# Newton iterations for reciprocal square roots: the iterate in columns of the PSUM tile just summed

## The chip, the cores and the metric

The kernel runs on one core of a Trainium2 chip. Its engines are TensorE (PE; its weight loads are shown apart as PEld), VectorE (DVE), ScalarE (ACT) and GpSimd (POOL); SyncE (SP) issues most DMAs. The metric is the device time of one execution in microseconds (us), the median of several runs. A profile is one more execution, taken by the hardware profiler.

## What is computed

Two transformer blocks of two layers each, on 512 tokens of 1024 features, in float32. Reciprocal square roots stand in every normalisation: of the residual stream, of the heads' queries and keys, and of the mixers' outputs. Cut to these:

```
def rmsnorm(x, g):
    xf = x.astype(jnp.float32)
    y = xf * lax.rsqrt(jnp.mean(xf * xf, axis=-1, keepdims=True) + EPS)
    return (y * g.astype(jnp.float32)).astype(x.dtype)

def l2norm(x):
    return x * lax.rsqrt(jnp.sum(x * x, axis=-1, keepdims=True) + EPS)
...
        qa = apply_grid_rope(rmsnorm(qa.reshape(b, s, A_HEADS, A_HEAD_DIM), q_norm_g[l]), cos, sin)
...
        qd = l2norm(qd.reshape(b, s, DN_HEADS, DN_DK)) * (DN_DK ** -0.5)
...
def _memory_cross_attention(h, mem_h, w_q, w_kv, q_norm_g, k_norm_g, w_o):
    q = _rms(_split_heads(h @ w_q, XA_HEADS), q_norm_g)
    mk, mv = _split_cols(mem_h @ w_kv, (XA_HEADS * XA_HD, XA_HEADS * XA_HD))
    mk = _rms(_split_heads(mk, XA_HEADS), k_norm_g)
```

The ten phases follow one another: mix and feed-forward twice (first block), then an even mixer, cross-attention, feed-forward, an odd mixer, cross-attention, feed-forward (second block).

## The kernel before

Activations lie with features on the 128 partitions and the 512 tokens along the free dimension. Each weight piece is split into a high and a low part: ScalarE casts it to whi (L474), GpSimd subtracts to get wlo (`tt` with engine gpsimd, L383), and three matmuls make one product (L487, L490, L491, in `proj`) into the PSUM tiles psb, or ps. Four pieces of each part are in flight (pool `whl`).

A reciprocal root takes this path. Squares are made by ScalarE. `tok_sums` transposes four (or two) 128-token pieces of them on TensorE into a PSUM tile ps (L412), and VectorE adds up each row (L416), so that a token stands on a partition and a root is one column: 4 columns for a norm, up to 32 where several heads and tiles share a chain. `rsqrt` then forms 1/sqrt(scale*x + eps) on VectorE, with a shift and a subtraction on the bits as the first guess and three Newton steps: 12 instructions on 2 to 32 columns, each waiting for the one before. Its working tile is called rsq, its result rc, or nrc for a norm of the residual stream, or rso for the delta rule's output. `spread` (L455) transposes the columns back over all partitions on TensorE. `rs_cols` does sums and root for a head's vectors; where these are of a still unnormalised projection, `r` is the norm, and the sums are first multiplied by its squared root (rc2) and the result by its root (rc).

`Norm.chunk` runs once for each of eight feature tiles of the residual stream; the last call forms the sums, nrc, its square and the spread copy rB (L303), which scales the projections as they leave PSUM (`pad<-psb,rB`, `x<-psb,rB`). There are ten norms, and 64 chains in all: ten of norms, two of rso, 52 of `rs_cols`.

In cross-attention (`_cross`) the root of the queries, rq, scales the row maximum and the exponentials (L1721, ScalarE), which VectorE then divides by their sum (L1726) before TensorE transposes them (L1728); the root of the memory, mrc, scales the values as ScalarE copies them from PSUM (L1699). In mix, two chains of 16 columns (`queries`, first and second group) run beside `solve`, the triangular inverse whose products ntmp and sums N are VectorE's, and beside the attention core, whose exponentials (L956) need the roots. `l2` makes two chains of 32 columns beside the convolution (kq, L697). PSUM tiles come from rings: `pss`, `psf` and `psg` with one to four buffers a phase, psb with two. A scheduler that knows a cost for each instruction orders each engine's instructions ahead of time; the engines then run them in that order.

Of the kernel before, what the change touches and what calls it, by code (L numbers as in the profile page):

```python
# [11 lines left out]
F32 = mybir.dt.float32  # L12
F32R = mybir.dt.float32r
I32 = mybir.dt.int32
AF = mybir.ActivationFunctionType
ALU = mybir.AluOpType
# [4 lines left out]
P = 128  # L21
S = 512
D = 1024
DEPTH = 2
EPS = 1e-6
# [79 lines left out]
NVEC, _ = _vec_layout()  # L105
# [155 lines left out]
class Norm:  # L261
# [10 lines left out]
    def chunk(self, m):  # L272
        k, nc = self.k, self.k.nc
        a = k.actp.tile([P, 2, S], F32R, name="act", tag="act")
        gcol = k.vec(self.g, m)
        nc.scalar.activation(a[:, 0], k.x[m], AF.Copy, scale=gcol)
        lo = nc.vector.scalar_tensor_tensor(a[:, 1], k.x[m], gcol, a[:, 0].bitcast(F32), ALU.mult, ALU.subtract)  # L277
        self.acts[m] = a
        sq = k.nrm.tile([P, S], F32, name="nsq", tag="nsq", bufs=2) if self.n else k.nrm.tile([P, S], F32, name="ssq", tag="ssq")
        if self.first and m in (1, 3, 5):  # L280
            k.tt(sq, k.x[m], k.x[m], ALU.mult, "gpsimd")
        else:
            self.last = lo, nc.scalar.activation(sq, k.x[m], AF.Square)
        self.n += 1

        if self.n == 1:
            self.acc = sq
        elif self.n < 8:
            k.tt(self.acc, self.acc, sq, ALU.add, "vector" if self.first else "gpsimd")
        if self.n == 7:  # L290
            self.sums = k.nrm.tile([P, 2, 4], F32, name="nsum", tag="nsum", bufs=2)
            k.tok_sums(self.sums[:, 0], self.acc)
        if self.n == 8:
            k.tok_sums(self.sums[:, 1], sq)
            k.tt(self.sums[:, 0], self.sums[:, 0], self.sums[:, 1], ALU.add)

            self.rc = k.nrm.tile([P, 4, 1], F32, name="nrc", tag="nrc", bufs=2)
            self.rc2 = k.nrm.tile([P, 4, 1], F32, name="nrc2", tag="nrc2", bufs=2)
            k.rsqrt(self.rc.rearrange("p t c -> p (t c)"), self.sums[:, 0], 1.0 / D, EPS)
            k.tt(self.rc2, self.rc, self.rc, ALU.mult)  # L300
            ps = k.spread(self.rc)
            self.r = k.nrm.tile([P, S], F32, name="rB", tag="rB")
            nc.scalar.copy(self.r, ps)  # L303


class Prog:
# [75 lines left out]
    def tt(self, out, a, b, op, eng="vector"):  # L382
        getattr(self.nc, eng).tensor_tensor(out, a, b, op)  # L383

    def rsqrt(self, out, in_, scale, eps):


        nc = self.nc
        n = out.shape[-1]
        y = self.nrm.tile([P, 2, 32], F32, name="rsq", tag="rsq", bufs=4)  # L390
        v, u = y[:, 0, :n], y[:, 1, :n]
        nc.vector.tensor_scalar(v, in_, scale, eps, ALU.mult, ALU.add)
        nc.vector.tensor_scalar(u.bitcast(I32), v.bitcast(I32), 1, None, ALU.logical_shift_right)
        nc.vector.tensor_scalar(out.bitcast(I32), u.bitcast(I32), -1.0, float(0x5F3759DF), ALU.mult, ALU.add)
        for _ in range(3):
            self.tt(u, out, out, ALU.mult)
            nc.vector.scalar_tensor_tensor(u, u, -0.5, v, ALU.mult, ALU.mult)  # L397
            nc.vector.scalar_tensor_tensor(out, u, 1.5, out, ALU.add, ALU.mult)

    def issue_behind(self, ins, before):  # L400

# [4 lines left out]
    def tok_sums(self, out, sq, view=None, nt=4, psum=None):  # L406


        nc = self.nc
        ps = (psum or self.pss)()  # L410
        for t in range(nt):
            nc.tensor.transpose(ps[:, t * P:(t + 1) * P], sq[:, t * P:(t + 1) * P], self.ident)  # L412
        v = ps[:, :nt * P].rearrange("p (t d) -> p t d", t=nt)
        if view is not None:
            v = view(v)
        nc.vector.tensor_reduce(out, v, AX.X if len(v.shape) == len(out.shape) + 1 else AX.XY, ALU.add)  # L416

    def rs_cols(self, groups, view, ncol, scale, eps, nt=4, psum=None, r=None):

        nc = self.nc
        n = nt * ncol
        rc = self.nrm.tile([P, 32], F32, name="rc", tag="rc", bufs=4)
        sums = self.nrm.tile([P, 32], F32, name="sums", tag="sums", bufs=4)
        ng = 0
        for sq in groups:
            self.tok_sums(sums[:, ng * n:(ng + 1) * n].rearrange("p (t c) -> p t c", t=nt), sq, view, nt, psum)
            ng += 1
        by_tok = lambda t: t[:, :n * ng].rearrange("p (g t c) -> p g t c", g=ng, t=nt)  # L430
        of = lambda t: t.unsqueeze(1).broadcast_to((P, ng, nt, ncol))
        if r is not None:
            self.tt(by_tok(sums), by_tok(sums), of(r.rc2), ALU.mult)
        self.rsqrt(rc[:, :n * ng], sums[:, :n * ng], scale, eps)
        if r is not None:
            self.tt(by_tok(rc), by_tok(rc), of(r.rc), ALU.mult)
        return [rc[:, g * n:(g + 1) * n].rearrange("p (t c) -> p t c", t=nt) for g in range(ng)]

    def all_features(self, v):
# [202 lines left out]
    def _mix(self, l, nm, nxt, mp):  # L642
        nc, tc = self.nc, self.tc
# [87 lines left out]
        ps = self.pss()  # L731
# [5 lines left out]
        ps = self.pss()  # L737
# [26 lines left out]
        ps = self.pss()  # L764
# [10 lines left out]
        ps = self.pss()  # L775
# [490 lines left out]
        rso = mp.tile([P, 32], F32, name="rso")  # L1266
        for b in range(4):
            sq = r3.tile([P, S], F32, name="osq", tag="osq", bufs=2)
            nc.scalar.activation(sq, oacc[b], AF.Square)
            nc.vector.tensor_reduce(rso[:, b * 8:b * 8 + 8], sq.rearrange("p (u d) -> p u d", d=64), AX.X, ALU.add)  # L1270

        self.rsqrt(rso, rso, 4.0 / 64, 4.0 * EPS)
        for b in range(4):
            self.tt(oacc[b].rearrange("p (u d) -> p u d", d=64), oacc[b].rearrange("p (u d) -> p u d", d=64),
                    rso[:, b * 8:b * 8 + 8].unsqueeze(2).broadcast_to((P, 8, 64)), ALU.mult)
# [1 line left out]
        for pp in range(2):  # L1277
            o = [r3.tile([P, S], F32, name="of", tag="of", bufs=4) for h in range(2)]
            for b in range(2):
                ps = self.pss()  # L1280
# [3 lines left out]
                for h in range(2):  # L1284
                    v = lambda t: t[:, tk].rearrange("p (c x) -> p c x", c=4)
# [5 lines left out]
        for m, _ in enumerate(branch(self.A["wod"][l], ydn, gt1)):  # L1291
            self.tt(gt1[m], gt1[m], gt0[m], ALU.add, "gpsimd")
            t = r3.tile([P, 2, S], F32R, name=f"mx{m}")
# [496 lines left out]
```

## Time and profile before

| | |
|---|---|
| median of 3 runs | 3457.84 us (3456.24 to 3459.11) |
| the profiled execution's own time | 3445.89 us |
| its span, first to last instruction | 3444.1 us |
| TensorE's mean granted clock | 0.979 |
| VectorE busy | 2030.8 us (59%) |
| GpSimd busy | 1806.1 us (52%) |
| ScalarE busy | 1483.2 us (43%) |

A busy share is over the whole span. VectorE and GpSimd count as busy while an instruction of theirs is under way, whether it computes or is held up: a long duration on few columns is a wait that shows as busy time. The granted clock is 1.0 at 2.4 GHz and 0.5 at 1.2 GHz.

### The profile page before, as it was taken

How to read it: one execution, taken by the hardware profiler on the slowest of the kernel's cores; microseconds unless marked ns; L12 is line 12 of the kernel's file. 1: busy time of each engine (PE TensorE's matmuls, PEld its weight loads, DVE VectorE, ACT ScalarE, POOL GpSimd, SP SyncE). 2: the span in 40 equal slices, each digit the busy share in tenths (PEclk: the TensorE clock that was granted, in tenths of full speed). 3: DMA queues.
4: the chain of work that ended last, by engine and by line, in shares of the span. 5: the costliest groups of instructions: out<-in, count | busy, mean ns of one | idle time of the engine just before them, and what ended most of it. 6: DMA issues, size and time to landing. Idle time of an engine off the chain costs nothing. (4 is left out here: it accounts for less than half of the span.)

```text
span 3444.1 us, 46891 instructions
## 1 busy us (share of the span) xinstructions
PE 3227.7 (94%) x17342; PEld 2655.6 (77%) x17342; DVE 2030.8 (59%) x3571; ACT 1483.2 (43%) x2766; POOL 1806.1 (52%) x1493
## 2 busy tenths in 40 slices
PE   8888899999987889999999898999999998999999
PEld 6666778888766667788877776878888887888887
DVE  8988555554698866464466676553223786653222
ACT  4526534343553553443353325443334444544332
POOL 4653365444565434654456556565556335555554
PEclk9999999999998999999999998999999999999999
DMA  4532542222354234222232113223223212222222
GB/s 148 160 89 62 119 127 98 98 89 92 121 158 124 73 81 133 100 99 92 98 112 86 62 47 103 85 99 121 94 98 107 78 67 101 88 87 98 98 97 87
DMA packets 135869, 342.53 MB, mean 99 GB/s; under 512 B 43056, under 2 KB 80304, under 8 KB 106969
## 3 DMA queue, kind: packets, MB, share of 16 engines
q1 hardware_dynamic: 134208, 336.04, 30.5%
q10 hardware_dynamic: 1432, 3.49, 0.4%
q8 instruction: 138, 2.26, 0.3%
q14 instruction: 91, 0.74, 0.1%
HBM read 312.15 MB, written 29.97 MB: 99 GB/s over the span
## 5 line engine op out<-in xcount | busy, mean ns | idle before, releaser
L383 POOL TENSOR_TENSOR wlo<-wraw,whi 128x512 fp32r<-128x512 f32 (+2 forms) x1044 | 1369.1, 1316 | 1397.9 <-ACT whi L474 1359.6
L474 ACT CAST whi<-wraw 128x512 fp32r<-128x512 f32 (+2 forms) x1044 | 631.5, 608 | 1129.5 <-PE psb L490 835.2
L487 PE MATMUL psb<-act,whi 128*128 128x512 f32 x1888 | 758.8, 402 | 59.6 <-DVE x L383 19.6
L491 PE MATMUL psb<-act,wlo 128*128 128x512 f32 x1888 | 751.5, 399 | 3.2 <-POOL wlo L383 3.0
L490 PE MATMUL psb<-act,whi 128*128 128x512 f32 x1888 | 752.6, 399 | 0.8 <-DVE act L277 0.6
L487 PEld LDWEIGHTS psb<-act,whi 128*128 128x128 f32 x1888 | 363.5, 193 | 140.0 <-issue 43.4
L491 PEld LDWEIGHTS psb<-act,wlo 128*128 128x128 f32 x1888 | 362.2, 192 | 81.1 <-POOL wlo L383 5.6
L490 PEld LDWEIGHTS psb<-act,whi 128*128 128x128 f32 x1888 | 363.4, 192 | 75.0 <-DVE act L277 2.3
L383 DVE TENSOR_TENSOR x<-psb,x 128x512 f32<-128x512 f32 x168 | 115.2, 689 | 377.0 <-PE psb L491 376.6
L487 PE MATMUL ps<-act,whi 128*128 128x512 f32 (+1 forms) x720 | 280.7, 390 | 3.4 <-ACT rB L303 3.4
L491 PE MATMUL ps<-act,wlo 128*128 128x512 f32 (+1 forms) x720 | 280.2, 389 | 0.0
L490 PE MATMUL ps<-act,whi 128*128 128x512 f32 (+1 forms) x720 | 280.2, 389 | 0.0
L487 PE MATMUL psb<-mid,whi 128*128 128x512 f32 x704 | 276.7, 394 | 1.0 <-DVE x L383 1.0
L491 PE MATMUL psb<-mid,wlo 128*128 128x512 f32 x704 | 276.2, 392 | 0.0
L490 PE MATMUL psb<-mid,whi 128*128 128x512 f32 x704 | 273.6, 389 | 0.0
L487 PEld LDWEIGHTS ps<-act,whi 128*128 128x128 f32 (+1 forms) x720 | 133.9, 186 | 33.7 <-ACT rB L303 4.6
L491 PEld LDWEIGHTS ps<-act,wlo 128*128 128x128 f32 (+1 forms) x720 | 133.9, 186 | 29.4
L490 PEld LDWEIGHTS ps<-act,whi 128*128 128x128 f32 (+1 forms) x720 | 133.9, 186 | 29.1
L491 PEld LDWEIGHTS psb<-mid,wlo 128*128 128x128 f32 x704 | 132.1, 188 | 30.5
L487 PEld LDWEIGHTS psb<-mid,whi 128*128 128x128 f32 x704 | 132.3, 188 | 29.3 <-DVE x L383 1.5
L490 PEld LDWEIGHTS psb<-mid,whi 128*128 128x128 f32 x704 | 132.1, 188 | 29.5
L383 DVE TENSOR_TENSOR cv<-ps,cv 128x512 f32<-128x512 f32 (+1 forms) x60 | 41.5, 692 | 175.9 <-PE ps L491 106.5
(437 smaller groups left out, 5712.3 us busy)
## 6 DMA issues: line engine op xcount, KB each, us to landing
wraw<-in_wup SPq DMA_DIRECT2D x44, 1024.0 KB, 4.8
wraw<-in_fup SPq DMA_DIRECT2D x44, 1024.0 KB, 4.8
wraw<-in_win SPq DMA_DIRECT2D x38, 1024.0 KB, 5.0
wraw<-in_wdn SPq DMA_DIRECT2D x16, 1024.0 KB, 4.8
wraw<-in_evin SPq DMA_DIRECT2D x16, 1024.0 KB, 4.8
wraw<-in_xakv SPq DMA_DIRECT2D x16, 1024.0 KB, 4.9
wraw<-in_fdn SPq DMA_DIRECT2D x16, 1024.0 KB, 4.8
wraw<-in_odin SPq DMA_DIRECT2D x12, 1024.0 KB, 4.9
```

Of the source, the lines that this page charges most:

```text
L383: getattr(self.nc, eng).tensor_tensor(out, a, b, op)
L474: nc.scalar.copy(hi, part)
L487: mm = nc.tensor.matmul(ps, hi[:, i], acts[k][:, 0, :n], start=k == 0, stop=False)
L490: nc.tensor.matmul(ps, hi[:, i], acts[k][:, 1, :n], start=False, stop=False)
L491: nc.tensor.matmul(ps, lo[:, i], acts[k][:, 0, :n], start=False, stop=k == kc - 1)
```

## The change

`rsqrt` takes the PSUM tile that `tok_sums` has just summed (for rso a fresh one) and keeps the iterate y in its first columns. The bits' shift goes from SBUF into PSUM, the subtraction runs in PSUM, and each Newton step is written so that of its two sources one (v or u) is in SBUF and one (y) in PSUM: u = -0.5 v y, u = u y, y = (u + 1.5) y. The last step writes to SBUF; where a norm's root has to be multiplied in (`r`), it stays in PSUM and that product moves it out. The first instruction, v = scale*x + eps, is as before. The square rc2 of a norm's root is now made by ScalarE.

```
--- before.py
+++ after.py
@@ -291,13 +291,13 @@
             self.sums = k.nrm.tile([P, 2, 4], F32, name="nsum", tag="nsum", bufs=2)
             k.tok_sums(self.sums[:, 0], self.acc)
         if self.n == 8:
-            k.tok_sums(self.sums[:, 1], sq)
+            ps = k.tok_sums(self.sums[:, 1], sq)
             k.tt(self.sums[:, 0], self.sums[:, 0], self.sums[:, 1], ALU.add)
 
             self.rc = k.nrm.tile([P, 4, 1], F32, name="nrc", tag="nrc", bufs=2)
             self.rc2 = k.nrm.tile([P, 4, 1], F32, name="nrc2", tag="nrc2", bufs=2)
-            k.rsqrt(self.rc.rearrange("p t c -> p (t c)"), self.sums[:, 0], 1.0 / D, EPS)
-            k.tt(self.rc2, self.rc, self.rc, ALU.mult)
+            k.rsqrt(self.rc.rearrange("p t c -> p (t c)"), self.sums[:, 0], 1.0 / D, EPS, ps)
+            nc.scalar.activation(self.rc2, self.rc, AF.Square)
             ps = k.spread(self.rc)
             self.r = k.nrm.tile([P, S], F32, name="rB", tag="rB")
             nc.scalar.copy(self.r, ps)
@@ -382,20 +382,23 @@
     def tt(self, out, a, b, op, eng="vector"):
         getattr(self.nc, eng).tensor_tensor(out, a, b, op)
 
-    def rsqrt(self, out, in_, scale, eps):
+    def rsqrt(self, out, in_, scale, eps, ps, r=None):
 
 
         nc = self.nc
-        n = out.shape[-1]
-        y = self.nrm.tile([P, 2, 32], F32, name="rsq", tag="rsq", bufs=4)
-        v, u = y[:, 0, :n], y[:, 1, :n]
+        n = in_.shape[-1]
+        y = ps[:, :n]
+        t = self.nrm.tile([P, 2, 32], F32, name="rsq", tag="rsq", bufs=4)
+        v, u = t[:, 0, :n], t[:, 1, :n]
         nc.vector.tensor_scalar(v, in_, scale, eps, ALU.mult, ALU.add)
-        nc.vector.tensor_scalar(u.bitcast(I32), v.bitcast(I32), 1, None, ALU.logical_shift_right)
-        nc.vector.tensor_scalar(out.bitcast(I32), u.bitcast(I32), -1.0, float(0x5F3759DF), ALU.mult, ALU.add)
-        for _ in range(3):
-            self.tt(u, out, out, ALU.mult)
-            nc.vector.scalar_tensor_tensor(u, u, -0.5, v, ALU.mult, ALU.mult)
-            nc.vector.scalar_tensor_tensor(out, u, 1.5, out, ALU.add, ALU.mult)
+        nc.vector.tensor_scalar(y.bitcast(I32), v.bitcast(I32), 1, None, ALU.logical_shift_right)
+        nc.vector.tensor_scalar(y.bitcast(I32), y.bitcast(I32), -1.0, float(0x5F3759DF), ALU.mult, ALU.add)
+        for i in range(3):
+            nc.vector.scalar_tensor_tensor(u, v, -0.5, y, ALU.mult, ALU.mult)
+            self.tt(u, u, y, ALU.mult)
+            nc.vector.scalar_tensor_tensor(out if r is None and i == 2 else y, u, 1.5, y, ALU.add, ALU.mult)
+        if r is not None:
+            r(out, y)
 
     def issue_behind(self, ins, before):
 
@@ -414,6 +417,7 @@
         if view is not None:
             v = view(v)
         nc.vector.tensor_reduce(out, v, AX.X if len(v.shape) == len(out.shape) + 1 else AX.XY, ALU.add)
+        return ps
 
     def rs_cols(self, groups, view, ncol, scale, eps, nt=4, psum=None, r=None):
 
@@ -425,15 +429,14 @@
         sums = self.nrm.tile([P, 32], F32, name="sums", tag="sums", bufs=4)
         ng = 0
         for sq in groups:
-            self.tok_sums(sums[:, ng * n:(ng + 1) * n].rearrange("p (t c) -> p t c", t=nt), sq, view, nt, psum)
+            ps = self.tok_sums(sums[:, ng * n:(ng + 1) * n].rearrange("p (t c) -> p t c", t=nt), sq, view, nt, psum)
             ng += 1
         by_tok = lambda t: t[:, :n * ng].rearrange("p (g t c) -> p g t c", g=ng, t=nt)
         of = lambda t: t.unsqueeze(1).broadcast_to((P, ng, nt, ncol))
         if r is not None:
             self.tt(by_tok(sums), by_tok(sums), of(r.rc2), ALU.mult)
-        self.rsqrt(rc[:, :n * ng], sums[:, :n * ng], scale, eps)
-        if r is not None:
-            self.tt(by_tok(rc), by_tok(rc), of(r.rc), ALU.mult)
+        times = lambda out, y: self.tt(by_tok(out), by_tok(y), of(r.rc), ALU.mult)
+        self.rsqrt(rc[:, :n * ng], sums[:, :n * ng], scale, eps, ps, times if r is not None else None)
         return [rc[:, g * n:(g + 1) * n].rearrange("p (t c) -> p t c", t=nt) for g in range(ng)]
 
     def all_features(self, v):
@@ -1269,7 +1272,7 @@
             nc.scalar.activation(sq, oacc[b], AF.Square)
             nc.vector.tensor_reduce(rso[:, b * 8:b * 8 + 8], sq.rearrange("p (u d) -> p u d", d=64), AX.X, ALU.add)
 
-        self.rsqrt(rso, rso, 4.0 / 64, 4.0 * EPS)
+        self.rsqrt(rso, rso, 4.0 / 64, 4.0 * EPS, self.pss())
         for b in range(4):
             self.tt(oacc[b].rearrange("p (u d) -> p u d", d=64), oacc[b].rearrange("p (u d) -> p u d", d=64),
                     rso[:, b * 8:b * 8 + 8].unsqueeze(2).broadcast_to((P, 8, 64)), ALU.mult)
```

The order of VectorE's instructions in the first phase of cross-attention, second head, from the scaled sum on (ps is the PSUM tile just summed, nrc the norm's squared root or root), before:

```order
L383 TENSOR_TENSOR sums<-sums,nrc_18251 128x4
L392 TENSOR_SCALAR rsq<-sums 128x4
L393 TENSOR_SCALAR rsq<-rsq 128x4
L394 TENSOR_SCALAR rc<-rsq 128x4
L383 TENSOR_TENSOR rsq<-rc 128x4
L397 SCALAR_TENSOR_TENSOR rsq<-rsq 128x4
L398 SCALAR_TENSOR_TENSOR rc<-rsq,rc 128x4
L383 TENSOR_TENSOR rsq<-rc 128x4
L397 SCALAR_TENSOR_TENSOR rsq<-rsq 128x4
L398 SCALAR_TENSOR_TENSOR rc<-rsq,rc 128x4
L383 TENSOR_TENSOR rsq<-rc 128x4
L397 SCALAR_TENSOR_TENSOR rsq<-rsq 128x4
```

and now:

```order
L383 TENSOR_TENSOR sums<-sums,nrc_18253 128x4
L393 TENSOR_SCALAR rsq<-sums 128x4
L394 TENSOR_SCALAR ps_19348<-rsq 128x4
L395 TENSOR_SCALAR ps_19348<-ps_19348 128x4
L397 SCALAR_TENSOR_TENSOR rsq<-rsq,ps_19348 128x4
L383 TENSOR_TENSOR rsq<-rsq,ps_19348 128x4
L399 SCALAR_TENSOR_TENSOR ps_19348<-rsq,ps_19348 128x4
L397 SCALAR_TENSOR_TENSOR rsq<-rsq,ps_19348 128x4
L383 TENSOR_TENSOR rsq<-rsq,ps_19348 128x4
L399 SCALAR_TENSOR_TENSOR ps_19348<-rsq,ps_19348 128x4
L397 SCALAR_TENSOR_TENSOR rsq<-rsq,ps_19348 128x4
L383 TENSOR_TENSOR rsq<-rsq,ps_19348 128x4
```

No instruction has changed its place here; eleven of twelve have an operand in PSUM, and so has the product with nrc that follows.

VectorE in the first mix layer, the roots of the queries' first group (16 columns) beside the triangular solve (N, ntmp), from the scaled sum on, before:

```order
L383 TENSOR_TENSOR sums<-sums,nrc_166 128x16
L383 TENSOR_TENSOR ntmp<-N 128x440
L392 TENSOR_SCALAR rsq<-sums 128x16
L383 TENSOR_TENSOR N<-N,ntmp 128x2x11x20
L393 TENSOR_SCALAR rsq<-rsq 128x16
L383 TENSOR_TENSOR ntmp<-N 128x456
L394 TENSOR_SCALAR rc<-rsq 128x16
L383 TENSOR_TENSOR N<-N,ntmp 128x2x12x19
L383 TENSOR_TENSOR rsq<-rc 128x16
L383 TENSOR_TENSOR x<-psb,rB 128x512
L383 TENSOR_TENSOR ntmp<-N 128x468
L397 SCALAR_TENSOR_TENSOR rsq<-rsq 128x16
```

and now:

```order
L383 TENSOR_TENSOR sums<-sums,nrc_166 128x16
L383 TENSOR_TENSOR ntmp<-N 128x440
L393 TENSOR_SCALAR rsq<-sums 128x16
L383 TENSOR_TENSOR N<-N,ntmp 128x2x11x20
L394 TENSOR_SCALAR ps_1860<-rsq 128x16
L383 TENSOR_TENSOR ntmp<-N 128x456
L395 TENSOR_SCALAR ps_1860<-ps_1860 128x16
L383 TENSOR_TENSOR N<-N,ntmp 128x2x12x19
L397 SCALAR_TENSOR_TENSOR rsq<-rsq,ps_1860 128x16
L383 TENSOR_TENSOR x<-psb,rB 128x512
L383 TENSOR_TENSOR ntmp<-N 128x468
L383 TENSOR_TENSOR rsq<-rsq,ps_1860 128x16
```

Up to the product x<-psb,rB every instruction keeps its neighbours; after it the solve's ntmp and the step change only in what the step is. Further on the attention's row maxima and solve's products change places by a few rows.

ScalarE at the norm that opens the first feed-forward (whi casts of weights, rB the spread root), before:

```order
L474 CAST whi<-wraw 128x512 x2
L276 ACTIVATE act<-x,vect 128x512
L283 ACTIVATE nsq<-x 128x512
L474 CAST whi<-wraw 128x512 x4
L303 COPY rB<-ps_5151 128x512
L587 ACTIVATE cv<-pad_5168,vect 128x512
L474 CAST whi<-wraw 128x512
```

and now:

```order
L477 CAST whi<-wraw 128x512 x2
L276 ACTIVATE act<-x,vect 128x512
L283 ACTIVATE nsq<-x 128x512
L477 CAST whi<-wraw 128x512 x3
L300 ACTIVATE nrc_5137<-nrc 128x4
L477 CAST whi<-wraw 128x512
L303 COPY rB<-ps_5152 128x512
L590 ACTIVATE cv<-pad_5169,vect 128x512
L477 CAST whi<-wraw 128x512
```

The square of nrc stands ahead of the last weight cast before the copy rB.

## Rows read from the trace of the kernel before

**Rows 1.** The page's part 1, TensorE's matmuls: busy us, share of the span, instructions.

```profile
PE 3227.7 (94%) x17342; PEld 2655.6 (77%) x17342; DVE 2030.8 (59%) x3571; ACT 1483.2 (43%) x2766; POOL 1806.1 (52%) x1493
```

**Rows 2.** Whom TensorE waited for: us in total, times, longest us.

```profile
PE ps L1728 <- DVE pr L1726: 12.6, 6, 3.0
PE psb L487 <- ACT kx L1699: 7.5, 3, 4.2
PE psb L487 <- ACT sq L1638: 7.0, 1, 7.0
```

**Rows 3.** Instructions on tile rsq: count, duration ns min/median/max, first and last start, forms.

```profile
L397 DVE SCALAR_TENSOR_TENSOR rsq<-rsq x192: 142/163/1282, 26.1 to 3088.3; 128x4 f32<-128x4 f32 x126, 128x2 f32<-128x2 f32 x30, 128x32 f32<-128x32 f32 x18, 128x16 f32<-128x16 f32 x12
```

**Rows 4.** Instructions on tile rsq over the whole span: stretch, VectorE's busy us and count.

```profile
0.00:3445.00 3445.00, 271.03 (x768) 0.98 0.31 99
```

**Rows 5.** Timelines of GpSimd and VectorE at 2146 us: start us, us, instruction.

```profile
2146.01 5.04 POOL L383 TENSOR_TENSOR wlo<-wraw,whi 128x512 fp32r<-128x512 f32 x4
...
2147.34 1.22 DVE L397 SCALAR_TENSOR_TENSOR rsq<-rsq 128x2 f32<-128x2 f32 x1
```

**Rows 6.** Instructions on tile pad, and on tile cv (columns as rows 3).

```profile
L383 DVE TENSOR_TENSOR pad<-psb,rB x112: 675/686/694, 29.0 to 3401.6; 128x512 f32<-128x512 f32 x112
...
L383 DVE TENSOR_TENSOR cv<-cv x44: 678/1185/1671, 562.7 to 1755.9; 128x512 f32<-128x512 f32 x44
```

**Rows 7.** Timelines of VectorE and TensorE, cross, 2172 to 2181 us; in brackets idle before.

```profile
2172.45 1.21 DVE L394 TENSOR_SCALAR rc<-rsq 128x4 int32<-128x4 int32 x1
...
2180.30 0.70 PE L1728 MATMUL ps<-cstt,pr 128*128 128x128 f32 x4 [2.96 <-DVE pr L1726]
```

**Rows 8.** Timelines of VectorE and TensorE, first cross phase, 2122 to 2130 us.

```profile
2122.66 2.56 DVE L393 TENSOR_SCALAR rsq<-rsq 128x4 int32<-128x4 int32 x2
2125.14 1.38 DVE L394 TENSOR_SCALAR rc<-rsq 128x4 int32<-128x4 int32 x2
...
2129.11 0.58 PE L487 MATMUL psb<-mact,whi 128*128 128x256 f32 x1 [4.22 <-ACT kx L1699]
```

**Rows 9.** Timelines of VectorE and TensorE, second cross phase, 2899 to 2923 us.

```profile
2899.85 1.18 DVE L393 TENSOR_SCALAR rsq<-rsq 128x4 int32<-128x4 int32 x1
2917.09 1.35 DVE L398 SCALAR_TENSOR_TENSOR rc<-rsq,rc 128x4 f32<-128x4 f32 x2
...
2922.14 0.39 PE L487 MATMUL psb<-mact,whi 128*128 128x256 f32 x1 [2.86 <-ACT kx L1699]
```

**Rows 10.** Timelines of TensorE and VectorE in the first mix layer.

```profile
80.23 0.76 PE L487 MATMUL psb<-act,whi 128*128 128x512 f32 x1 [2.81 <-DVE pad L383]
...
127.52 0.66 PE L455 MATMUL ps<-cstt,rce 128*128 128x128 f32 x4 [1.44 <-DVE rce L449]
...
227.71 1.23 DVE L383 TENSOR_TENSOR rsq<-rc 128x16 f32<-128x16 f32 x1
...
229.68 0.47 PE L487 MATMUL psb<-act,whi 128*128 128x512 f32 x1 [3.28 <-DVE x L383]
...
321.16 0.66 PE L959 MATMUL ps<-cstt,th 128*128 128x128 f32 x4 [2.81 <-ACT th L956]
```

**Rows 11.** Timeline of TensorE at a norm's end, 1434.65 us.

```profile
1434.65 0.62 PE L455 MATMUL ps<-cstt,nrc 128*128 128x128 f32 x4 [0.29 <-DVE nrc L398]
```

**Rows 12.** Stretches in cross, in mix: us, TensorE busy, granted clock; sums of 5, of 6.

```profile
2128.00:2134.80 6.80, 5.66 (x25) 0.50 0.40 137
...
sum 23.80, PE 21.91; mean PE 4.38
...
sum 20.40, PE 20.03; mean PE 3.34
```

**Rows 13.** Timeline of VectorE, a chain without late steps, 26 us.

```profile
26.07 0.16 DVE L397 SCALAR_TENSOR_TENSOR rsq<-rsq 128x4 f32<-128x4 f32 x1
26.27 0.16 DVE L398 SCALAR_TENSOR_TENSOR nrc<-rsq,nrc 128x4 f32<-128x4 f32 x1
```

**Rows 14.** Instructions on tile el (columns as rows 3): ScalarE's smallest activation of four columns.

```profile
L1445 ACT ACTIVATE el<-cum x4: 202/206/209, 1808.7 to 1977.5; 128x4 f32<-128x4 f32 x4
```

## The prediction

> **What bounds the kernel now.** The busy shares come first: TensorE's matmuls fill 94% of the span [rows 1], so what can be won is its idle time and the stretches at half clock. Next comes the list of whom TensorE waited for [rows 2]: three of its entries end in the cross-attention phases, 12.6 us on the softmax's scaling, 7.5 us on ScalarE's copy that carries the memory's root, 7.0 us on a square. None names the root itself. To see why the roots are behind them, read the root's own tile: a step of its Newton loop takes 163 ns in the middle of 192 and 1282 ns at most, on the same few columns [rows 3], and the 768 instructions on that tile keep VectorE busy for 271 us [rows 4]; at 163 ns each they would need about 125.
>
> Where the long ones come from is seen by laying two engines' timelines side by side. While GpSimd makes four wlo tiles without a break (5.04 us), the Newton steps follow each other at 1.2 us, one for each GpSimd instruction, though each has two columns to do [rows 5]. Steps that take half a microsecond or more are called late below. A step can only start between two of GpSimd's. The list by form tells which instructions this hits: of pad<-psb,rB, one operand in PSUM, none of 112 is above 694 ns; of cv<-cv, the same operation and size with both operands in SBUF, the median is 1185 and the longest 1671 ns [rows 6]. So what VectorE stands behind is a GpSimd instruction with SBUF operands, and only when its own two sources are both in SBUF.
>
> **The change, part by part.** Each chain had 12 instructions in SBUF alone; now the first still is, and the other 11 have an operand in PSUM. The first one, the sum's scaling by rc2 before it and the add of nsum stay exposed. The closing product with nrc now reads PSUM too. The order on VectorE is the old one step by step in cross; in mix the neighbours change places by a few rows.
>
> Cross, both phases. In the chain at 2172 us three steps like the one of 1.21 us and one of half that stand between the sum and the exponentials; TensorE then idles 2.96 us [rows 7]. At 0.2 us each the chain would end 3.5 us earlier, so the idle time goes: four such places, 4 x 2.96 = 11.8 of the 12.6 us. In the first phase the memory's root and the queries' root run interleaved, and four of their steps, 2.56 us for two and 1.38 for the next two, precede ScalarE's copy; TensorE idles 4.22 us [rows 8]. Two interleaved steps share 0.2 us where nothing is late, so 3.94 - 0.4 = 3.5 of it is theirs. In the second phase the same place has 2.86 us of idle time with three late pairs of steps ahead, the first 1.35 us: all of it, 2.9. The 7.0 us on the square has two late steps ahead, the first 1.18 us [rows 9]: 2.0. Together 20.2.
>
> Mix, each of two layers. Here late steps alternate with other two-SBUF instructions (the triangular solve's N and ntmp, the convolution's kq); whoever follows the freed step then stands behind the same GpSimd instruction, so I count nothing for those, and only steps that a PSUM reader or another step follows. L2 norms: 2.0 of the 2.81 us at 80 us and 1.4 of 1.44 at 127 us. Queries of the first group: a step of 1.23 us directly ahead of x<-psb,rB, for which TensorE idles 3.28 us; with two more such, 3.0. Queries of the second group: five late steps in a row, then 2.81 us of idle time: 2.8 [rows 10]. That is 9.2 a layer, 18.4 in all. The second layer's places read like the first's.
>
> Norm ends: five places like the 0.29 us for nrc [rows 11], 1.6 together; the 0.68 us for rB after it stays, since that is the spread and its copy. Odd layer and the feed-forwards: TensorE hardly idles there, so nothing, though their steps are as late.
>
> Sum without clock: 20.2 + 18.4 + 1.6 = 40 us.
>
> Clock: five stretches in cross, 23.8 us with TensorE busy for 21.9, were granted 0.50, which is 1.2 of 2.4 GHz, each beginning at the end of one of the idle times just named. If the idle time goes, work there takes half: up to 11 us. In mix another 20.4 us lie so behind the waits named there, busy for 20.0 [rows 12], but other stalls stay around them. Bounds 0 and (21.9 + 20.0) / 2 = 21; I take 10, cross nearly whole and nothing for mix.
>
> The price of PSUM steps: no row shows VectorE writing PSUM, and none a chain through it. In SBUF a free step follows the last after 0.20 us [rows 13]. Reading it costs nothing extra at equal size: 675 against 678 ns at best [rows 6]. The nearest rows thus say 0, and I take 0. A gain can be no more than the 0.04 us between one step's end and the next's start; the far bound of a loss is one more whole step, 0.20 us. What lies on the path is 21 places (8 cross, 8 mix, 5 norms) x 11 = 231 steps, so the bounds are 9 us won and 46 lost.
> The Trainium skill (Perfetto Trace Analysis, Optimizing Scalar/DVE Operations) gives VectorE about 60 ns of access overhead on SBUF and 125 on PSUM; by that each step would cost 65 ns more, 15 us as an estimate, and the sum would be a gain of 35. The rows on reads do not agree with it; no run here shows writes.
>
> rc2 on ScalarE: ten instructions leave VectorE (0.16 us each, two of them late), ten of about 0.2 us come to ScalarE, the price of an activation on 128x4 [rows 14]. At the norm ends one whi cast now stands behind it and so behind nrc; before, that cast ran at the time nrc was ready, and nrc comes earlier, so nothing. In the first cross phase a square of the queries stands behind it, 5 us after nrc: nothing.
>
> The PSUM buffer is held until the last step instead of the sum. The next user of that ring on TensorE is mostly the spread or a later tile that needs the root anyway: nothing.
>
> Forecast: a gain of 40 + 10 = 50 us. Against the profiled execution's own 3445.89 us that is 3396; the runs' median is 3457.84, 12 us above it, so **3408**.
>
> **Rivals.** (1) *The wait passes on.* VectorE reaches its next two-SBUF instruction sooner and stands behind the same GpSimd instruction there; a third of the 40 us is left and no clock: 3445. For it: in mix most late steps do stand ahead of such an instruction. Against: in cross the chain runs step after step and ends in a PSUM reader or an activation.
> (2) *Steps in PSUM are dearer by half a step*, 0.10 us: 231 x 0.10 = 23 us given back, 3431. The page named above would make it 3423.
> (3) *Slower: the write into PSUM has to land before the next step reads it.* Every step then waits for the one ahead; from 0.22 us a step on (50 / 231) the gain is gone, and at 0.35 us it is 81 - 50 = 31 us slower, 3489. For it: every chain step depends on the one before, and no row shows this. Against: PSUM is read at SBUF's pace [rows 6].
> (4) *It does not do what it says*: a step with one operand in PSUM still stands behind GpSimd: no change, 3458. Against it: 112 rows of pad.
> (5) *The held buffer*: sixteen roots in the odd layer, 2.35 us each if TensorE needed that buffer at once, 38 us given back: 3446. The order speaks against it.
>
> **How the numbers follow.** Forecast 0.67, (1) 0.10, (2) 0.09, (3) 0.06, (4) 0.06, (5) 0.02. Differences within 0.2%, 7 us, cannot be told from no change here. Faster: 0.67 + 0.10 + 0.09 + 0.02 = 0.88; same 0.06; slower 0.06. Range: low, all the clock and the small gain per step: 3458 - 40 - 21 - 9 = 3388; high, rivals (1) and (5): 3446. Left out are (3) and (4), 0.12.
>
> **What would show it.** The longest step on the root's tile below 0.35 us except in the first of each chain; VectorE's time on the tile near 140 us; the waits on the softmax's scaling at 1 us instead of 12.6; the five slow stretches in cross gone. Wrong it would be if steps with PSUM operands are longer than 0.25 us or begin more than 0.3 us apart, if late times appear on the kq, N or th instructions instead, or if TensorE's idle time moves to another releaser in the same places.

## The result, and the profile after

| | before | changed |
|---|---|---|
| median | 3457.04 us (4 runs, 3454.24 to 3459.11) | 3413.27 us (4 runs, 3410.85 to 3417.31) |
| ratio, 95% interval | | 0.9875, 0.9858 to 0.9892 |
| the profiled execution's own time | 3445.89 us | 3413.20 us |
| VectorE busy | 2030.8 us | 1916.1 us |
| TensorE's mean granted clock | 0.979 | 0.980 |

The change gains 44 us, 1.25%, with an interval of 37 to 49 us. In a later set, with fresh runs of both on one chip, it was 39 us (3455.03 to 3415.65, ratio 0.9885, 0.9867 to 0.9904).

The page's part 1 of the changed kernel, to be held against [rows 1]: GpSimd's work is the same, VectorE has 115 us less.

```profile
PE 3218.6 (94%) x17342; PEld 2653.0 (78%) x17342; DVE 1916.1 (56%) x3561; ACT 1486.3 (44%) x2776; POOL 1808.2 (53%) x1493
```

Instructions on the tile rsq in the changed kernel (count, duration ns min/median/max), to be held against [rows 3]:

```profile
L397 DVE SCALAR_TENSOR_TENSOR rsq<-rsq,ps x192: 138/157/188, 25.9 to 3053.8; 128x4 f32<-128x4 f32 x126, 128x2 f32<-128x2 f32 x30, 128x32 f32<-128x32 f32 x18, 128x16 f32<-128x16 f32 x12
...
L399 DVE SCALAR_TENSOR_TENSOR ps<-rsq,ps x166: 150/166/197, 26.2 to 3053.6; 128x4 f32<-128x4 f32 x108, 128x2 f32<-128x2 f32 x28, 128x32 f32<-128x32 f32 x12, 128x16 f32<-128x16 f32 x12
L394 DVE TENSOR_SCALAR ps<-rsq x64: 144/166/196, 25.5 to 3052.3; 128x4 int32<-128x4 int32 x42, 128x2 int32<-128x2 int32 x10, 128x32 int32<-128x32 int32 x6, 128x16 int32<-128x16 int32 x4
L393 DVE TENSOR_SCALAR rsq<-sums x52: 152/170/1257, 69.9 to 3001.8; 128x4 f32<-128x4 f32 x32, 128x2 f32<-128x2 f32 x10, 128x32 f32<-128x32 f32 x4, 128x16 f32<-128x16 f32 x4
```

The subtraction, which has PSUM on both sides, stands under its own line:

```profile
L395 DVE TENSOR_SCALAR ps<-ps x64: 153/170/200, 25.7 to 3052.5; 128x4 int32<-128x4 int32 x42, 128x2 int32<-128x2 int32 x10, 128x32 int32<-128x32 int32 x6, 128x16 int32<-128x16 int32 x4
```

The middle of the list has hardly moved (163 to 157 ns); the far end has: no step with an operand in PSUM takes more than 200 ns, where [rows 3] had 1282. Only the first instruction of each chain, still in SBUF alone, is late as before (1257). VectorE's time on the tile, one row for the whole span, answers to [rows 4]; 64 of the 768 instructions now touch PSUM only and are not in it:

```profile
0.00:3450.00 3450.00, 121.30 (x704) 0.98 0.31 99
```

Comparing start times of VectorE and GpSimd says the same without any average. Of the instructions on rsq that began well inside a GpSimd product (0.1 us after its start or later, and 0.3 us or more before its end), the kernel before has 95 besides the first of a chain, and all 95 took more than 0.3 us. The changed kernel has 241, and none took 0.2 us.

Whom TensorE waited for in the changed kernel (us in total, times, longest us), to be held against [rows 2]:

```profile
PE ps L952 <- DVE rc L383: 7.2, 2, 3.6
...
PE ps L1731 <- DVE pr L1729: 6.6, 8, 0.8
...
PE psb L490 <- ACT sq L1641: 5.2, 1, 5.2
...
PE ps L458 <- DVE rc L383: 4.1, 2, 2.2
...
PE ps L458 <- DVE nrc L399: 0.9, 1, 0.9
...
PE psb L490 <- ACT kx L1702: 0.6, 2, 0.3
```

The softmax's scaling fell from 12.6 to 6.6 us, the copy with the memory's root from 7.5 to 0.6, the square from 7.0 to 5.2. Two waits for rc are new or nearly so: 7.2 us in mix, and 4.1 in cross where 0.4 stood.

By place, from the start of one copy rB to the start of the next (each profile has ten, one a phase), for two profiles of each kernel (the second of each is from the experiments):

| stretch, us | before | changed |
|---|---|---|
| mix, first layer | 522.6, 522.3 | 516.3, 516.0 |
| mix, second layer | 523.2, 525.4 | 515.1, 514.7 |
| even mixer | 313.6, 314.9 | 314.5, 314.4 |
| cross, first | 182.6, 185.1 | 173.1, 176.5 |
| odd mixer | 247.0, 245.6 | 245.0, 245.2 |
| cross, second | 179.0, 177.7 | 171.9, 171.8 |
| the rest (start, four feed-forwards) | 1476.2, 1477.7 | 1475.7, 1475.7 |
| span | 3444.1, 3448.8 | 3411.4, 3414.2 |

By the means of the two, cross gives 15.6 us, mix 15.8, the odd mixer 1.2, and the start and the feed-forwards together 1.3.

### The profile page after: what moved, and what is told of

Same layout as the page of the kernel before. It is cut to its first block, busy times and chain, and to the rows that moved or that the text cites. A ratio compares the mean times of both kernels' runs of the same rounds, so it can differ in the third digit from the quotient of the medians.

```text
span 3411.4 us, 46902 instructions
## 1 busy us (share of the span) xinstructions
PE 3218.6 (94%) x17342; PEld 2653.0 (78%) x17342; DVE 1916.1 (56%) x3561; ACT 1486.3 (44%) x2776; POOL 1808.2 (53%) x1493
```

## The experiments

The theory: a VectorE instruction with all its operands in SBUF stands behind a running GpSimd instruction, one with an operand in PSUM does not, and the whole gain comes from that. The rivals: the rewritten steps, or the new order of instructions that came with them, help by themselves.

**The new algebra in SBUF.** The iterate goes into a third row of rsq, and the norm's square back to VectorE:

```
-        y = ps[:, :n]
-        t = self.nrm.tile([P, 2, 32], F32, name="rsq", tag="rsq", bufs=4)
-        v, u = t[:, 0, :n], t[:, 1, :n]
+        t = self.nrm.tile([P, 3, 32], F32, name="rsq", tag="rsq", bufs=4)
+        v, u, y = t[:, 0, :n], t[:, 1, :n], t[:, 2, :n]
```

> The changed kernel with the iterate y in a third row of the tile rsq in SBUF and the norm's square back on VectorE; the steps' new algebra (u = -0.5 v y, u = u y, y = (u + 1.5) y) stays. Theory (a step is held behind a GpSimd instruction only while all its operands are in SBUF): no gain, 3457 within 7 us, the longest step on rsq at 1.2 to 1.3 us as before, VectorE's time on that tile 250 us or more. Rival (the new algebra, or the order that comes with it, is what helps): near the changed kernel's 3413, and the late steps rarer.

Measured: 3457.46 us against 3456.82, ratio 1.0006 (0.9997 to 1.0016). Its instructions on rsq, first two rows:

```profile
L396 DVE SCALAR_TENSOR_TENSOR rsq<-rsq x192: 142/164/1282, 25.9 to 3092.5; 128x4 f32<-128x4 f32 x126, 128x2 f32<-128x2 f32 x30, 128x32 f32<-128x32 f32 x18, 128x16 f32<-128x16 f32 x12
L383 DVE TENSOR_TENSOR rsq<-rsq x192: 142/163/1289, 26.1 to 3092.7; 128x4 f32<-128x4 f32 x126, 128x2 f32<-128x2 f32 x30, 128x32 f32<-128x32 f32 x18, 128x16 f32<-128x16 f32 x12
```

The late steps are back in full, and the algebra is worth nothing. The order of instructions is not tested by this run: in its trace VectorE's instructions stand in the order of the kernel before (3567 of 3571 in the same sequence), while in the changed kernel 54 instructions, besides the ten squares, have moved.

**One part of the kernel alone.** A flag set by phase sends all other chains, and the norms, through the old steps (for mix alone it names "m0" and "m1"):

```
+            k.in_psum = p in ("xa0", "xa1")
...
+        if ps is None or not self.in_psum:
+            y = self.nrm.tile([P, 2, 32], F32, name="rsq", tag="rsq", bufs=4)
...
+            return
```

> The iterate in PSUM only for the chains of the two cross-attention phases, all others and the norms by the old steps, the norm's square on VectorE. Theory (the profiles put 9.5 and 7.1 us of the gain into the cross phases): a gain of 14 to 22 us, 3435 to 3443, with the waits for the softmax's scaled exponentials at 6.6 us in all. Rival (the gain hangs on mix, and cross gives back what it wins as a later wait): less than 8 us.

> The iterate in PSUM only for the chains of the two mix layers (rso's among them), all others and the norms by the old steps, the norm's square on VectorE. Theory (the profiles put 6.4 and 8.1 us into these layers, with 3 late waits that pass on): a gain of 10 to 20 us, 3437 to 3447; with cross alone it adds up to the whole 44 within 10. Rival (in mix the wait only passes to the solve's and the convolution's instructions): within 7 us of 3457.

Measured: cross alone 3438.93 us, ratio 0.9952 (0.9939 to 0.9965), a gain of 12 to 21 us; mix alone 3435.68, ratio 0.9945 (0.9932 to 0.9958), 15 to 24 us. The waits for the softmax's scaling, with cross alone and then with mix alone:

```profile
PE ps L1744 <- DVE pr L1742: 6.5, 8, 0.8
```

```profile
PE ps L1744 <- DVE pr L1742: 13.0, 7, 3.0
```

Each wait follows the chain of its own phase. The two gains, by their ratios 16.6 and 19.0 us, sum to 36, within 10 of the whole.

**The norm's square back on VectorE.**

```
-            nc.scalar.activation(self.rc2, self.rc, AF.Square)
+            k.tt(self.rc2, self.rc, self.rc, ALU.mult)
```

> The changed kernel with the norm's squared root made by VectorE again. Theory (ten squares, off the path): 3413 within 5 us. Rival (the square held up to 1.1 us behind GpSimd delays the first sums of the next phase, or it matters that ScalarE has one more instruction ahead of the copy rB): 5 to 12 us away from 3413, slower by the first, faster by the second.

Measured: 3409.21 us, ratio 0.9872 (0.9857 to 0.9887), which cannot be told from the change's 0.9875. The square's place is worth nothing that shows.

**GpSimd's subtraction left out**, in the kernel before and in the changed one. The third matmul of each product takes the high part again, so the low part of the weights is missing from the result:

```
-            self.tt(lo, part, hi.bitcast(F32), ALU.subtract, "gpsimd")
-            return k, hi, lo
+            return k, hi, hi
```

> The kernel before without GpSimd's subtraction for the weights' low part (the third matmul of each product takes the high part again, so the low part is left out of the result): GpSimd loses 1044 of its 1493 instructions and some 1370 us. Theory (the steps were held by GpSimd's instructions): the steps on rsq fall to about 0.2 us but for the few beside what GpSimd still has, VectorE's time on that tile to 125 to 160 us, and this kernel and the changed one without the same subtraction differ by no more than 10 us, below 0.3%. Rival (the gain comes from PSUM, the algebra or the order themselves): the two differ by about 44 us as with it.

> The changed kernel without GpSimd's subtraction for the weights' low part (left out of the result). Theory: within 10 us of the kernel before with the same left out. Rival: about 44 us quicker than that.

Measured: 3316.70 and 3304.94 us; of the 44 us 12 are left, just beyond the 10 that the theory allowed. The page's part 1 and the time on rsq, kernel before without the subtraction:

```profile
PE 3182.8 (96%) x17342; PEld 2634.6 (79%) x17342; DVE 1677.9 (51%) x3571; ACT 1486.4 (45%) x2766; POOL 434.6 (13%) x449
...
0.00:3300.00 3300.00, 149.83 (x768) 0.99 0.32 103
```

By place, the two cross phases now differ by 0.3 and 0.2 us (161.2 and 161.0; 161.4 and 161.6), mix still by 8.8 and 4.0. So in cross the gain hangs on GpSimd's subtractions. In mix either GpSimd's other products there or the changed order was left as an explanation, and the next pair tells them apart.

**GpSimd's products beside mix's chains moved to VectorE as well** (five such lines, in both kernels, on top of the edit before):

```
-            self.tt(q, q, rope[:, 0], ALU.mult, "gpsimd")
+            self.tt(q, q, rope[:, 0], ALU.mult)
```

> The kernel before without the weights' low part (left out of the result), and with the five GpSimd products of mix that run beside its chains (s, x twice, th, qa; 76 us a layer) moved to VectorE. Theory (of the 12 us that the pair without the low part still differed by, all in mix, the cause is what GpSimd still did there): with it gone this kernel and the changed one with the same edits differ by less than 5 us, and the longest step on rsq in mix is below 0.3 us. Rival (the new order of TensorE and VectorE in mix is worth 10 us by itself): still 8 to 15 us apart.

> The changed kernel with the same two edits (the weights' low part is left out of the result). Theory: within 5 us of the kernel before with them. Rival: 8 to 15 us quicker than that.

Measured: 3310.77 and 3311.22 us. The gain is gone. The kernel before with these edits, part 1 of its page and its slowest kind of step (elsewhere GpSimd still has 307 us of work, and a few steps are held by that):

```profile
PE 3185.4 (96%) x17342; PEld 2639.5 (80%) x17342; DVE 1673.1 (51%) x3661; ACT 1487.6 (45%) x2766; POOL 306.5 (9%) x359
...
L397 DVE SCALAR_TENSOR_TENSOR rsq<-rsq x192: 149/163/501, 23.9 to 2955.3; 128x4 f32<-128x4 f32 x126, 128x2 f32<-128x2 f32 x30, 128x32 f32<-128x32 f32 x18, 128x16 f32<-128x16 f32 x12
```

With little for VectorE to stand behind, the change is worth nothing: neither PSUM, nor the algebra, nor the order of instructions gives or costs anything that shows. In mix this is less clean than in cross, since VectorE has the moved products to do: the changed kernel's two mix layers are 5.0 and 4.7 us longer than with the subtraction alone left out, the kernel before's 4.6 and 0.2 us shorter.

**The sums in PSUM too.** The changed kernel leaves three SBUF-only instructions at the head of a chain. VectorE and TensorE in its first cross phase:

```profile
2111.37 1.19 DVE L383 TENSOR_TENSOR mrc<-mrc 128x2 f32<-128x2 f32 x1
2112.48 0.41 DVE L419 TENSOR_REDUCE sums<-ps 128x2 f32<-128x256 f32 x1
2112.93 0.88 DVE L383 TENSOR_TENSOR sums<-sums,mrc 128x2 f32<-128x2 f32 x1
2113.84 0.67 DVE L393 TENSOR_SCALAR rsq<-sums 128x2 f32<-128x2 f32 x1
2114.54 0.16 DVE L394 TENSOR_SCALAR ps<-rsq 128x2 int32<-128x2 int32 x1
...
2117.00 0.40 PE L458 MATMUL ps<-cstt,rc 128*128 128x128 f32 x2 [1.94 <-DVE rc L383]
```

GpSimd has a block of four subtractions from 2108.8 to 2113.8, and the square mrc and the scaled sum stand behind it; the third, at 2113.84, stands behind the product vt<-kx,vt that follows the block. This version takes them out of SBUF alone:

```
-            self.tt(by_tok(sums), by_tok(sums), of(r.rc2), ALU.mult)
+                self.tt(cols(ps), cols(ps), r.rc2.broadcast_to((P, nt, ncol)), ALU.mult)
+            self.nc.vector.tensor_scalar(t2[:, 0, ng * n:(ng + 1) * n], ps[:, :n], scale, eps, ALU.mult, ALU.add)
...
-        self.tt(mr.rc2, mr.rc, mr.rc, ALU.mult)
+        nc.scalar.activation(mr.rc2, mr.rc, AF.Square)
```

with `tok_sums` reducing into `ps[:, :n]`.

> The changed kernel, and the sums too are left in the PSUM tile: the reduction writes into the first columns of the tile it reads, the scaling by the squared root and v = scale*x + eps read them there (v for each group apart), and the memory's root is written to its tile by the last step and squared by ScalarE. Theory (the three SBUF-only instructions left at the head of a chain, 1.19, 0.88 and 0.67 us in the first cross phase, now carry the waits of 1.94 and 2.18 us on rc): those two waits fall below 0.6 us, a few more in mix, 5 to 15 us quicker than the changed kernel, 3398 to 3408. Rival (what is won passes to the next two-SBUF instruction, or the held PSUM buffer costs it): within 5 us of 3413 or slower.

Measured: 3408.20 us, ratio 0.9870 (0.9856 to 0.9885), inside the theory's range but not to be told from the change. So both were run on one chip:

> The changed kernel once more, beside the version with the sums in PSUM on the same chip: 3413 within 5 us, a ratio of 0.986 to 0.989.

> The version with the sums and the memory's root in PSUM once more. Theory (its first profile shows the two waits on rc gone, 1.4 and 0.7 us left of them, and no late step in any chain but rso's): 4 to 11 us quicker than the changed kernel on the same chip, a ratio of 0.984 to 0.9865. Rival (the 10 us between the two first profiles are the scatter of single executions): within 3 us of the changed kernel.

Measured: the changed kernel 3415.65 us, ratio 0.9885 (0.9867 to 0.9904); this version 3404.75, ratio 0.9858 (0.9838 to 0.9878). The intervals against the kernel before overlap, but the runs hardly do: 3410.82 to 3418.00 against 3401.78 to 3411.20. Its first instruction of a chain, which reads PSUM now, and the waits where the 4.1 us on rc had been:

```profile
L439 DVE TENSOR_SCALAR rsq<-ps x68: 140/155/167, 62.1 to 2991.5; 128x4 f32<-128x4 f32 x32, 128x8 f32<-128x8 f32 x26, 128x2 f32<-128x2 f32 x10
```

```profile
PE psb L495 <- ACT kx L1707: 2.7, 3, 1.8
```

No row for rc in cross remains; part of its time came back as a wait for kx, which stands next. By the medians of this set the version is 11 us quicker than the change and 50 us quicker than the kernel before; in the first set, where it ran without the change beside it, it was 44 us quicker than the kernel before, as the change is. By place (means of two profiles each) the difference is 5.6 us in cross, 3.7 in mix and 3.3 in the odd mixer.

**The kernel before once more.**

> The kernel before, unchanged, for a second profile of it: its first one took 3445.89 us, 12 us under the runs' median, while the changed kernel's profiled execution sits on its median. If that was one quick execution, this profile shows 3450 to 3462 us, and the 11 us more are found in the same waits or at half clock. If a profile of this kernel is always quicker, it shows 3446 again.

Measured: median 3451.09 us against 3452.03, and a profiled execution of 3450.62. Single executions of this kernel spread from 3445 to 3467 us over all sets, so the first profile was a quick one. The 5 us more of this second profile have no one place: the first cross phase, the second mix layer, the even mixer and the start are 1 to 2.5 us longer, the odd mixer and the second cross phase 1.3 us shorter (table above).

## Why the prediction was right, and where its sizes were off

The forecast was 3408 us and the range 3388 to 3446; 3413 was measured. The mechanism stands: the late steps were GpSimd's doing, an operand in PSUM ends them, and steps through PSUM are no dearer. Two of the signs that it named did not come: the waits on the softmax's scaling are at 6.6 us, not at 1, and slow stretches are left in cross. Its reading that VectorE stands behind GpSimd only when both its sources are in SBUF was too narrow: the late steps of [rows 8] and [rows 9], L393 and L394, have one source. The sum did not rest on that, for it took those steps as late all the same. Rivals (2) and (3) fall to two rows of a chain without late steps in the changed kernel: a write to PSUM and the step that reads it lie 0.20 us apart, as in [rows 13].

```profile
26.83 0.17 DVE L399 SCALAR_TENSOR_TENSOR ps<-rsq,ps 128x4 f32<-128x4 f32 x1
27.03 0.16 DVE L397 SCALAR_TENSOR_TENSOR rsq<-rsq,ps 128x4 f32<-128x4 f32 x1
```

By the figures of the Trainium skill (Perfetto Trace Analysis, Optimizing Scalar/DVE Operations) these steps were estimated to be longer by 65 ns; by the medians, 157 and 166 against 163 ns, they are not, and the measurement decides. Rival (4) falls to the list of rsq. Rival (5) left no trace where it was put: the odd mixer is 1.2 us shorter, not 38 longer. The held buffer does show in mix (below).

**Cross, 20.2 us of waits: mis-sized.** The four waits on the softmax's scaling were to go. They halved, from 12.6 to 6.6 us. The chain did end early; what the step left out is who comes next. Timelines of VectorE, ScalarE, TensorE and GpSimd at the place that answers to [rows 7]:

```profile
2155.55 0.23 DVE L383 TENSOR_TENSOR mx<-mx,rc 128x2 f32<-128x2 f32 x2
...
2159.49 1.63 DVE L1729 TENSOR_SCALAR pr<-pr,mx 128x256 f32<-128x256 f32 x2
...
2155.53 1.31 ACT L477 CAST whi<-wraw 128x512 fp32r<-128x512 f32 x2 [1.67 <-POOL sq L383]
2156.75 0.56 ACT L1724 ACTIVATE pr<-ps,mx,rc 128x256 f32<-128x256 f32 x1
...
2159.10 1.23 PE L1731 MATMUL ps<-cstt,pr 128*128 128x128 f32 x6 [0.81 <-DVE pr L1729]
2161.17 0.44 PE L1731 MATMUL ps<-cstt,pr 128*128 128x128 f32 x2 [0.84 <-DVE pr L1729]
...
2159.62 2.63 POOL L383 TENSOR_TENSOR wlo<-wraw,whi 128x512 fp32r<-128x512 f32 x2 [0.86 <-ACT whi L477]
```

The root and mx are ready at 2155.8, but ScalarE is in two weight casts until 2156.8; then come four exponentials; and the last two scalings, from SBUF to SBUF, take 1.63 us, since GpSimd's subtraction began beside them. Where 2.96 + 0.39 us of idle time stood, 0.81 + 0.84 stand now. The 0.39 in the kernel before:

```profile
2181.39 0.70 PE L1728 MATMUL ps<-cstt,pr 128*128 128x128 f32 x4 [0.39 <-DVE pr L1726]
```

The copies with the memory's root were costed at 3.5 and 2.9 us: those waits went (7.5 to 0.6), but waits of 1.94 and 2.18 us for rc stand 3 us later, from the head of the next chain. The step named two of these SBUF-only instructions as exposed, the scaled sum and the first of the chain, and gave them no price; the square of the memory's root it did not name. The 7.0 us on the square of the queries were costed at 2.0 and gave 1.8.

**Clock, 10 us: mis-sized.** Three stretches at half clock are left in cross where [rows 12] had five. The changed kernel's, with TensorE's busy time first and the granted clock near the end of each row:

```profile
2098.10:2101.50 3.40, 3.40 (x16) 3.40 (x17) 0.75 (x1) 2.25 (x5) 3.40 (x3) 0.50 0.00 0
2900.20:2903.60 3.40, 3.40 (x19) 3.40 (x18) 0.76 (x2) 1.86 (x5) 1.29 (x2) 0.51 0.06 27
2944.60:2948.00 3.40, 3.38 (x9) 2.80 (x10) 2.65 (x13) 0.66 (x2) 1.78 (x2) 0.50 0.40 80
```

Busy time at half clock fell from 21.9 to 10.2 us, and half of the difference, 5.9 us, is what the clock gave back in this pair of profiles. In the second profiles six such stretches are left of the kernel before and five of the changed one, and the same reckoning gives 2.5 us. Their sums, before and changed:

```profile
sum 23.80, PE 21.82; mean PE 3.64
```

```profile
sum 17.00, PE 16.90; mean PE 3.38
```

So of the 10 us taken, 2.5 to 5.9 came. Cross as a whole was forecast at 30 us and gave 15.6.

**Mix, 18.4 us: nearly right in sum, by other terms.** It gave 15.8. The 2.81 us at the second group of queries is 0.72, as told. At the L2 norms 2.81 us is 0.62, but at the next wait, for rce, 0.28 us became 2.85, so the matmul there starts only 1.16 us earlier. Before, then changed:

```profile
86.14 1.06 PE L455 MATMUL ps<-cstt,rce 128*128 128x128 f32 x8 [0.28 <-DVE rce L449]
```

```profile
78.03 0.47 PE L490 MATMUL psb<-act,whi 128*128 128x512 f32 x1 [0.62 <-DVE pad L383]
84.98 1.94 PE L458 MATMUL ps<-cstt,rce 128*128 128x128 f32 x8 [2.85 <-DVE rce L452]
...
313.00 0.66 PE L962 MATMUL ps<-cstt,th 128*128 128x128 f32 x4 [0.72 <-ACT th L959]
```

At the queries of the first group, costed at 3.0, rival (1) is what happened. VectorE there, and TensorE at the end:

```profile
221.11 0.16 DVE L394 TENSOR_SCALAR ps<-rsq 128x16 int32<-128x16 int32 x1
221.22 1.61 DVE L383 TENSOR_TENSOR ntmp<-N 128x456 f32<-128x456 f32 x1
222.76 0.17 DVE L395 TENSOR_SCALAR ps<-ps 128x16 int32<-128x16 int32 x1
222.87 1.57 DVE L383 TENSOR_TENSOR N<-N,ntmp 128x456 f32<-128x456 f32 x1
...
239.39 0.16 DVE L383 TENSOR_TENSOR rc<-ps,nrc 128x16 f32<-128x16 f32 x1
...
219.95 0.63 PE L952 MATMUL ps<-ka,qa 128*128 128x512 f32 x1
...
239.70 0.77 PE L952 MATMUL ps<-ka,qa 128*128 128x512 f32 x1 [3.62 <-DVE rc L383]
```

Each step is free, and the solve's instruction after it stands behind GpSimd in its place, so the chain still moves on by one step in 1.6 us: from the scaled sum to the product with nrc it takes 21.8 us, where it took 23.6.

The wait of 3.62 us at its end is another term, which the prediction put at nothing: the held PSUM buffer. The matmul at 239.70 makes attention scores from ka and qa and reads no root. It writes a tile of the ring from which the chain's tile ps comes, and it is released by the product that reads the iterate for the last time. In the changed kernel two score products run before the chain is done (the second at 219.95) and the third waits; in the kernel before, three ran while the chain was under way:

```profile
223.92 0.39 PE L949 MATMUL ps<-ka,qa 128*128 128x512 f32 x1
```

That is the wait for rc of 7.2 us in the two layers. It stands with the same 7.2 us in the version with mix alone, and in no version whose chains in mix run in SBUF. What it costs of the whole is not shown; no run freed the buffer earlier.

**Norm ends, 1.6 us: right.** The waits for nrc fell from 2.5 us in six places to 0.9 in one.

**The sum.** Profile against profile the gain is 34 us by the means, not 50. The medians gave 44 and 39. So 3408 came near to 3413 in part by luck: the sum was 16 us too large by the profiles, and it was set against the runs' median, 12 us above the profile from which its terms were read; set against that profile's own time it would have given 3396. Where the 5 to 10 us between profiles and medians lie stays open.

## What to carry to other kernels

An instruction of few columns with a median of 163 ns and a maximum of 1282 is waiting, although the profile counts it as busy and no list of waits names it: read the spread of a tile's durations, and lay the other engine's timeline beside the longest. A chain of small VectorE instructions beside a GpSimd stream can have one operand of each step in PSUM at no price per step. Begin at the head of the chain, and price what stands next after it, for a freed step in front of another SBUF-only instruction only hands the wait on. Price the PSUM buffer too: it is held as long as the chain runs, and a matmul of the same ring may wait for it (3.6 us here, twice).

## What the runs showed of the hardware

A destination in PSUM is enough: the shift (L394) has its only source in SBUF and writes PSUM, and none of 64 is above 196 ns, though 15 began well inside a GpSimd product. In the kernel before, the shift from SBUF to SBUF took up to 1328 ns. It, and the first instruction of a chain there:

```profile
L393 DVE TENSOR_SCALAR rsq<-rsq x64: 149/171/1328, 25.5 to 3084.5; 128x4 int32<-128x4 int32 x42, 128x2 int32<-128x2 int32 x10, 128x32 int32<-128x32 int32 x6, 128x16 int32<-128x16 int32 x4
L392 DVE TENSOR_SCALAR rsq<-sums x52: 160/170/1258, 70.0 to 3034.0; 128x4 f32<-128x4 f32 x32, 128x2 f32<-128x2 f32 x10, 128x32 f32<-128x32 f32 x4, 128x16 f32<-128x16 f32 x4
```

The Trainium skill (SBUF — State Buffer, Who interferes with whom) says that a VectorE instruction with at most one SBUF input stays clear of GpSimd unless it runs in a mode that uses both ports; the shift into PSUM agrees with that. The first instruction of a chain, with one source in SBUF and its result in SBUF, is late in both kernels (1258 and 1257 ns); that fits only if it ran in such a mode, which no trace here shows.

How much VectorE stands behind GpSimd was not expected: with the weights' subtraction left out, VectorE's busy time for the same 3571 instructions falls from 2030.8 to 1677.9 us, so some 350 us of it was waiting, of which this change takes away 115. The chains' 768 instructions alone lost 140 us (276 to 136, those that touch PSUM only counted in); part of it came back on what stands next, such as ntmp and N of the solve, from 80.7 to 92.3 us.
